# Layer 1's output projection by token groups, and value tiles woven with the last query and key norms

## The chip, the core and the metric

The kernel runs on one core of a Trainium2 chip. The metric is the device time of one execution in microseconds (us). Three runs of the kernel before gave 2983.98, 2985.34 and 2985.49 us; the median is 2985.34. The engines of the core are named as in the profile: PE multiplies matrices, PEld loads its weights, DVE, ACT and POOL work on vectors, SP issues most of the transfers (DMA).

## What is computed

One inference step of a two-layer backbone, for 1024 latent tokens and 128 context tokens together (1152 columns), 1024 features, all in fp32. Layer 0 mixes tokens by pooling and latent attention, layer 1 by neighbourhood attention with 16 heads. Each layer ends with an mlp. Cut to layer 1, where the change lies:

```python
def na_latent(h, k_ctx, v_ctx, w_in, na_q_norm, na_k_norm, rel_bias, w_out):
    q, k, v = na_qkv(h, w_in, na_q_norm, na_k_norm)     # rms norm of each head's q and k
    attn = neighbourhood_attention(q, k, v, k_ctx, v_ctx, rel_bias).reshape(B, S, D_MODEL)
    return attn @ w_out
...
    xs = xs + g1_s * ms
    xs = xs + g2_s * channel_mixer(modulate(xs, norm_mlp[i], sh2_s, sc2_s), mlp1[i], mlp2[i])
```

The context tokens (`xp`) take the same path with plain attention and their own modulation.

## The kernel before

Activations lie with features on the 128 partitions and the 1152 tokens along the free dimension: `x` is 8 tiles of 128x1152. A chunk is 384 tokens (`CH`, three of them) or 288 (`HC`, four). Each fp32 product is made of three products of halves: every operand is split into a rounded high part and a low rest (`wh`, `wl` for weights, `oh`, `ol` for attention outputs), and `mm3` (L329 to L337) issues high x low, low x high, high x high. A tile of the projection over 4 of its 8 input blocks is thus 12 matmuls. A weight block is loaded by SP into `wr`, cast by ACT into `wh` (L160) and subtracted by DVE, or for some weights by POOL, into `wl` (L161); there are 3 buffers of `wr`, and 4 each of `wh` and `wl`.

Python code issues the instructions, partly through generators that `weave` advances in proportion (each with a number of steps). A scheduler of the framework then simulates the program and fixes the order on each engine. Each engine runs its queue in order. PSUM has three pools of banks: `pa` and `pb` with 3, `pc` with 2. SBUF tiles come from a pool `S` of slots, which `S.free` gives back.

The passages that the change touches, in order of time:

1. Queries and keys of layer 1. In four groups `g` of two head pairs each, L1244 and following make the raw products, `square_sum` and `head_rstd` the norm factors `r8h`, `r8l` of the three chunks, and then, for each chunk and each of four tiles, two matmuls (`bcast`, L707 and L708) spread the factors over 128 partitions in a `ps_b` bank, and DVE multiplies (L1266). At the end the results are split (L1270, L1271) and stored to `qd` and `kd`.
2. Values. `value_gen1` makes 36 tiles of 24 matmuls of 256 columns (L1427 to L1429), nine for each quarter of the weights `wv`, and copies them out with ACT (L1433). It is woven with `na_max` (L1320, L1321, L1323) of heads 0 and 1.
3. The heads. Head `h` makes scores `ps_st`, exponents `p`, and values `ps_pv`; `finish_values` copies the outputs of a head pair to `no` and the denominators to `den`, and `recip_pair` (L1082 to L1086) divides. All pairs but the last go to memory (`od`) and come back as `op`.
4. The output projection. In head 15, `split_acts` (L937, L938) splits the first four pairs, and `out_first` makes 24 tiles (8 output blocks, three chunks of 384) over the first four input blocks; `OA` = 8 of them are woven into head 15 after `OW` = 10 empty steps, `OB` = 6 follow while the last pair's division runs. `out_second` makes 32 tiles (four chunks of 288) over the other four. Each tile is added to `x` by DVE, with the gate (L342 in the first, L896 in the second; two instructions where a chunk crosses from latent to context tokens). After chunks 0 and 1 their norm statistics follow, and from chunk 2 on `operand_gen` makes the mlp's operands: modulated `hq` (L311), their products, and the split into `bh` (L352) and `bl` (L353).
5. The mlp. L446 to L448 are the first matmuls of its first product; its weights pass through ACT L419 and DVE or POOL L420.

Layer 0 already has its projection in the form that the change brings to layer 1: `split_groups` (L914, L915) and `out_group`, with the residual in L929.

Of the kernel before, what the change touches and what calls it, by code (L numbers as in the profile page):

```python
# [13 lines left out]
ALU = mybir.AluOpType  # L14
# [18 lines left out]
XS, PSH, OW, OA, OB = (11, 11, 12, 12, 13, 13, 14, 14), (14, 14, 15, 15), 10, 8, 6  # L33
# [57 lines left out]
def hybrid_kernel(ctx: ExitStack, tc: tile.TileContext, I, O):  # L91
# [783 lines left out]

    def out_first(layer, acts):
        for q in range(4):
            ws = wout_chunk(layer, 0, q)
            for mi in range(2):
                for ch in range(NCH):  # L880
                    ps = PS("ps_o")[:, :CH]
                    mm3(ps, ws[mi], acts, ch * CH, ch * CH + CH)
                    residual(x, 2 * q + mi, ch, ps, layer, 0)
                    yield

    def out_second(layer, acts):
        ws = [wout_chunk(layer, 1, q) for q in range(4)]
        st, right, ops, og = {}, [], {}, None
        for ch in range(4):
            for m in range(KD):  # L890
                if ch == 3 or ch == 2 and m in (3, 6):
                    next(og, None)
                ps = PS("ps_o", ("pa", "pc")[m % 2])[:, :HC]
                mm3(ps, ws[m // 2][m % 2], acts, ch * HC, ch * HC + HC)
                for a, b, i in chunk_parts(ch, HC):
                    nc.vector.scalar_tensor_tensor(x[m][:, a:b], ps[:, a - ch * HC:b - ch * HC], adav(layer, 2, m, i),  # L896
                                                   x[m][:, a:b], op0=ALU.mult, op1=ALU.add)
# [33 lines left out]

    def split_acts(ops):
        acts = []
        for o in ops:
            a = (S.alloc("oh", F32R), S.alloc("ol", F32R))
            acts.append(a)
            nc.vector.tensor_copy(a[0], o)  # L937
            nc.vector.tensor_sub(a[1], o, a[0])  # L938
            S.free(o)
        return acts  # L940

    def free_acts(acts):
        for a in acts:
            S.free(*a)
# [288 lines left out]
    r8 = S.alloc("r8h", F32R), S.alloc("r8l", F32R)  # L1233
    silu_load()
    for g in range(4):
# [16 lines left out]
        for ch in range(NCH):  # L1252
            cs = slice(ch * CH, ch * CH + CH)
            ps8 = PS("ps8", "pb")[0:8, :CH]
            for t in range(4):
                square_sum(ps8, t, raw[t][:, cs], t == 0, t == 3)
            head_rstd(ps8, 64, cs, nts[(NCH * g + ch) % 2], r8, rows)
        for ch in range(NCH):
            for t in range(4):
                wn = "naq" if t < 2 else "nak"  # L1260
                pp_ = pq if t < 2 else pk
                ps = PS("ps_b", "pb")[:, :CH]
                bcast(ps, t, r8, slice(ch * CH, ch * CH + CH), rows)
                for a, b, i in chunk_parts(ch):
                    o = pp_[:, pairs[t] * P:pairs[t] * P + P] if i else raw[t][:, a:b]
                    nc.vector.scalar_tensor_tensor(o, raw[t][:, a:b], V(wn), ps[:, a - ch * CH:b - ch * CH],  # L1266
                                                   op0=ALU.mult, op1=ALU.mult)
        for t in range(4):
# [388 lines left out]
```

## Time and profile before

| what | value |
|---|---|
| median of three runs | 2985.34 us |
| the profiled execution | 2996.6 us |
| its span | 2994.7 us |
| mean granted PE clock | 0.977 |

One execution was profiled; all durations below come from it. A timeline row gives start and duration in us, engine, line, operation, output and inputs, partitions x elements and, in brackets, the idle time before it and what ended that. The durations of matmuls overlap, so the distance from start to start is their cost. A row of the windows gives a stretch's bounds and length, busy time and count of instructions for PE, PEld, DVE, ACT and POOL, then PE's granted clock, the DMA share and GB/s.

### The profile page before, as it was taken

Reading aid. Unit: us, or ns where it says so; the run is one execution under the profiler, and the core shown is the slowest. Engines: PE = TensorE matmul, PEld = TensorE weight load, DVE = VectorE, ACT = ScalarE, POOL = GpSimd, SP = SyncE. Lnnn points to the kernel's source line nnn. Section 1 sums busy time; section 2 is a strip of 40 time slices with the busy share of each in tenths; the row PEclk is TensorE's granted clock in tenths of the full one; section 3 lists DMA queues with packets and bytes.
Section 4 is the critical chain, followed back from the end, with each engine's and each line's share of the span. In section 5 each row is a group of like instructions: output and inputs, shape, how many; then the busy total and the mean of one; then the engine's idle time right before and its main releaser. Section 6 shows DMA issues by size and latency. Waiting matters only on the chain. (4 is left out here: it accounts for less than half of the span.)

```text
span 2994.7 us, 46426 instructions
## 1 busy us (share of the span) xinstructions
PE 2909.3 (97%) x18302; PEld 2610.2 (87%) x18302; DVE 2151.7 (72%) x3923; ACT 1321.2 (44%) x2136; POOL 329.3 (11%) x238
## 2 busy tenths in 40 slices
PE   7999999999999999999999999998989999999999
PEld 4955666799999999999988897666989999999999
DVE  5977863477778899786898524667587678877775
ACT  5463444345355544354644423444244445453433
POOL 2004010141000020000221000111020000200000
PEclk9997999999999999999999999898989999999999
DMA  6527521222232344233555325775213222332322
GB/s 236 170 86 254 144 76 41 77 77 88 84 105 77 101 141 148 78 99 92 170 204 183 116 101 128 194 187 165 70 36 99 80 91 85 117 101 78 98 78 89
DMA packets 117435, 347.59 MB, mean 116 GB/s; under 512 B 16697, under 2 KB 37801, under 8 KB 117218
## 3 DMA queue, kind: packets, MB, share of 16 engines
q1 hardware_dynamic: 114674, 340.76, 36.9%
q0 software_dynamic: 2544, 3.87, 0.4%
q8 instruction: 144, 2.36, 0.3%
q14 instruction: 73, 0.60, 0.1%
HBM read 296.54 MB, written 46.85 MB: 115 GB/s over the span
## 5 line engine op out<-in xcount | busy, mean ns | idle before, releaser
L477 PE MATMUL ps<-mh,wl 128*128 128x288 f32 x2048 | 599.8, 294 | 0.0
L478 PE MATMUL ps<-mh,wh 128*128 128x288 f32 x2048 | 595.6, 295 | 0.0
L476 PE MATMUL ps<-ml,wh 128*128 128x288 f32 x2048 | 590.4, 295 | 2.6 <-DVE x L482 1.4
L446 PE MATMUL ps<-bl,wh 128*128 128x288 f32 x1792 | 534.4, 299 | 16.1 <-DVE bl L353 5.2
L447 PE MATMUL ps<-bh,wl 128*128 128x288 f32 x1792 | 530.9, 296 | 0.0
L448 PE MATMUL ps<-bh,wh 128*128 128x288 f32 x1792 | 529.2, 295 | 0.0
L477 PEld LDWEIGHTS ps<-mh,wl 128*128 128x128 f32 x2048 | 384.2, 188 | 0.1
L476 PEld LDWEIGHTS ps<-ml,wh 128*128 128x128 f32 x2048 | 380.1, 188 | 3.6 <-DVE x L482 1.4
L478 PEld LDWEIGHTS ps<-mh,wh 128*128 128x128 f32 x2048 | 382.4, 188 | 0.0
L482 DVE SCALAR_TENSOR_TENSOR x<-ps,ada,x 128x288 f32<-128x288 f32 (+2 forms) x640 | 270.8, 451 | 122.7 <-PE ps L478 121.5
L446 PEld LDWEIGHTS ps<-bl,wh 128*128 128x128 f32 x1792 | 337.9, 189 | 20.5 <-issue 9.3
L448 PEld LDWEIGHTS ps<-bh,wh 128*128 128x128 f32 x1792 | 339.7, 190 | 0.0
L447 PEld LDWEIGHTS ps<-bh,wl 128*128 128x128 f32 x1792 | 338.8, 189 | 0.2
L160 ACT CAST wh<-wr 128x1024 fp32r<-128x1024 f32 x188 | 197.1, 1049 | 190.2 <-PE ps L448 77.3
L419 ACT CAST wh<-s 128x512 fp32r<-128x512 f32 x256 | 146.1, 618 | 278.6 <-PE ps L478 194.9
L161 DVE TENSOR_TENSOR wl<-wr,wh 128x1024 fp32r<-128x1024 f32 x144 | 179.2, 1248 | 60.1 <-ACT wh L160 60.1
L200 DVE CUSTOM_DVE_ANT_0 trash<-wada,silu 128x1024 bf16<-128x1024 f32 x160 | 206.1, 1288 | 13.3 <-DMA wada<-in_wada 6.9
L419 ACT CAST wh<-wr 128x1024 fp32r<-128x1024 f32 (+1 forms) x128 | 106.9, 835 | 199.7 <-PE ps L478 135.7
L161 POOL TENSOR_TENSOR wl<-wr,wh 128x1024 fp32r<-128x1024 f32 x44 | 117.2, 2670 | 689.8 <-ACT wh L160 689.8
L420 DVE TENSOR_TENSOR wl<-s,wh 128x512 fp32r<-128x512 f32 x232 | 157.2, 709 | 3.7 <-ACT wh L419 1.5
L1115 PE MATMUL ps_pv<-p,vt 128*128 128x512 f32 x288 | 147.7, 596 | 0.1
L1074 DVE TENSOR_REDUCE stat<-ps_m 128x1 f32<-128x384 f32 x192 | 98.6, 551 | 65.2 <-PE ps_m L1073 64.9
(321 smaller groups left out, 6044.2 us busy)
## 6 DMA issues: line engine op xcount, KB each, us to landing
wr<-in_w SPq DMA_DIRECT2D x256, 512.0 KB, 3.7
wada<-in_wada SPq DMA_DIRECT2D x48, 512.0 KB, 3.5
wada<-in_wada0t SPq DMA_DIRECT2D x32, 512.0 KB, 3.7
wr<-in_win SPq DMA_DIRECT2D x24, 512.0 KB, 4.5
wr<-in_wout SPq DMA_DIRECT2D x24, 512.0 KB, 4.3
kk<-kd SPq DMA_DIRECT2D x32, 288.0 KB, 7.3
wadan<-in_wada SPq DMA_DIRECT2D x16, 512.0 KB, 8.8
ta<-in_bias_q SPq DMA_DIRECT2D x16, 512.0 KB, 4.4
```

The lines of the kernel that those rows point to most:

```text
L160: nc.scalar.copy(hi, r)
L161: (nc.gpsimd if e else nc.vector).tensor_sub(lo, r, hi)
L200: nc.vector.tensor_tensor_reduce(trash, r[:, :D], silu[i][:, :D], scale=1.0, scalar=0.0, op0=ALU.mult, op1=ALU.add, accum_out=a)
L419: nc.scalar.copy(h, src)
L420: (nc.gpsimd if j in EDGE and min(ps) in EDGE_POOL else nc.vector).tensor_sub(l, src, h)
L446: nc.tensor.matmul(ps, wh[:, a], hl[:, b], start=k == 0, stop=False)
L447: nc.tensor.matmul(ps, wl[:, a], hh[:, b], start=False, stop=False)
L448: nc.tensor.matmul(ps, wh[:, a], hh[:, b], start=False, stop=k == 3)
L476: nc.tensor.matmul(ps, wh, hl, start=kk == 0, stop=False)
L477: nc.tensor.matmul(ps, wl, hh, start=False, stop=False)
L478: nc.tensor.matmul(ps, wh, hh, start=False, stop=kk == 3)
L482: nc.vector.scalar_tensor_tensor(x[m][:, a:b], ps[:, a - ch * HC:b - ch * HC], g, x[m][:, a:b], op0=ALU.mult, op1=ALU.add)
```

## The change

First, the norms of a group become a generator `norm_group`, which yields after each chunk's factors, after each chunk's four multiplications and after each of four stores. `value_gen1` is defined ahead of the loop. For groups 0 to 2 the generator is run through as before; for the last group it is woven with the first nine value tiles. The other 27 value tiles are then woven with `na_max` of heads 0 and 1.

Second, layer 1's operands are split by `split_groups` into two halves of 576 tokens. `out_first` makes chunks 0 and 1 over the first four input blocks, 16 tiles of 288 columns; `OA` becomes 10. `out_second` makes the same two chunks over the other four blocks, with their norm statistics, then gives back the halves of group 0 it holds, and makes chunks 2 and 3 over all eight blocks, in tiles of 24 matmuls, with the weights of both halves loaded again; after every second of these 16 tiles `operand_gen` advances by one step. `split_acts` and `free_acts` go.

```diff
-XS, PSH, OW, OA, OB = (11, 11, 12, 12, 13, 13, 14, 14), (14, 14, 15, 15), 10, 8, 6
+XS, PSH, OW, OA, OB = (11, 11, 12, 12, 13, 13, 14, 14), (14, 14, 15, 15), 10, 10, 6
...
+    def out_tile(layer, m, ch, ws, acts, k):
+        ps = PS("ps_o", ("pa", "pc")[m % 2] if k else "pa")[:, :HC]
+        mm3(ps, ws, acts, ch % 2 * HC, ch % 2 * HC + HC)
+        for a, b, i in chunk_parts(ch, HC):
+            nc.vector.scalar_tensor_tensor(x[m][:, a:b], ps[:, a - ch * HC:b - ch * HC], adav(layer, 2, m, i),
+                                           x[m][:, a:b], op0=ALU.mult, op1=ALU.add)
...
     def out_first(layer, acts):
         for q in range(4):
             ws = wout_chunk(layer, 0, q)
             for mi in range(2):
-                for ch in range(NCH):
-                    ps = PS("ps_o")[:, :CH]
-                    mm3(ps, ws[mi], acts, ch * CH, ch * CH + CH)
-                    residual(x, 2 * q + mi, ch, ps, layer, 0)
+                for ch in range(2):
+                    out_tile(layer, 2 * q + mi, ch, ws[mi], acts, 0)
                     yield
...
     def out_second(layer, acts):
         ws = [wout_chunk(layer, 1, q) for q in range(4)]
-        st, right, ops, og = {}, [], {}, None
-        for ch in range(4):
+        st = {}
+        for ch in range(2):
             for m in range(KD):
-                if ch == 3 or ch == 2 and m in (3, 6):
-                    next(og, None)
...
-            if ch < 2:
-                st[ch] = norm_stats(x, ch, HC)
-            if ch == 1:
-                og = operand_gen(ops, quad_apply(x, 0, layer, st[0]), right)
-            elif ch == 2:
-                right.extend(quad_apply(x, 1, layer, st[1]))
+                out_tile(layer, m, ch, ws[m // 2][m % 2], [a[0] for a in acts[4:]], 1)
+            st[ch] = norm_stats(x, ch, HC)
+        for a in acts[4:]:
+            S.free_ap(a[0][0])
+        ops = {}
+        og = operand_gen(ops, quad_apply(x, 0, layer, st[0]), quad_apply(x, 1, layer, st[1]))
+        n = 0
+        for q in range(4):
+            ws = [wout_chunk(layer, half, q) for half in range(2)]
+            for mi in range(2):
+                for ch in (2, 3):
+                    out_tile(layer, 2 * q + mi, ch, [w for half in range(2) for w in ws[half][mi]], [a[1] for a in acts], 1)
+                    n += 1
+                    if n % 2 == 0:
+                        next(og, None)
         run(og)
...
+        norm = norm_group(g, raw, rows, pairs)
+        if g < 3:
+            run(norm)
+        else:
+            vg = value_gen1()
+            weave((norm, 10), (islice(vg, 9), 9))
...
-    weave((value_gen1(), 36), (chain(na_max(0, tls[0]), na_max(1, tls[1])), 10))
+    weave((vg, 27), (chain(na_max(0, tls[0]), na_max(1, tls[1])), 10))
...
-            acts = split_acts(pairs)
-            of = out_first(1, acts)
+            acts = [split_groups(o) for o in pairs]
+            of = out_first(1, [a[0] for a in acts])
...
-    free_acts(acts)
-    acts = split_acts(pairs + opairs[7:])
+    for a in acts:
+        S.free_ap(a[0][0])
+    acts += [split_groups(o) for o in pairs + opairs[7:]]
     ops = out_second(1, acts)
```

Lines of the changed kernel have other numbers: L1266 becomes L1247, L1427 to L1429 become L1278 to L1280, L1320 becomes L1356, L914 and L915 become L924 and L925, and the residual of layer 1 is L880.

The order of PE's instructions around the last norms, before the change, from the end of the seventh value tile on:

```order
L1428 MATMUL ps_v_16828<-wh,hl_956_13882 128x256
L1429 MATMUL ps_v_16828<-wh,hh_948_13874 128x256
L707 MATMUL ps_b<-r8h_14389,bcs_14365 128x384
L708 MATMUL ps_b<-r8l_14390,bcs_14365 128x384
...
L707 MATMUL ps_b<-r8h_14389,bcs_14365 128x384 x3
L708 MATMUL ps_b<-r8l_14390,bcs_14365 128x384 x3
L707 MATMUL ps_b<-r8h_14389,bcs_14365 128x384
L708 MATMUL ps_b<-r8l_14390,bcs_14365 128x384
L1320 MATMUL ps_m<-kk_16653,qq_16654 128x256
```

And at the same place after it, where `ps_v_16800` is the eighth value tile:

```order
L1279 MATMUL ps_v_16770<-wh,hl_956_13882 128x256
L1280 MATMUL ps_v_16770<-wh,hh_948_13874 128x256
L1278 MATMUL ps_v_16800<-wl,hh_941_13867 128x256
...
L1280 MATMUL ps_v_16800<-wh,hh_943_13869 128x256
L707 MATMUL ps_b<-r8h_14389,bcs_14365 128x384
L708 MATMUL ps_b<-r8l_14390,bcs_14365 128x384
L1278 MATMUL ps_v_16800<-wl,hh_944_13870 128x256
...
L1278 MATMUL ps_v_16800<-wl,hh_946_13872 128x256
L707 MATMUL ps_b<-r8h_14389,bcs_14365 128x384
L708 MATMUL ps_b<-r8l_14390,bcs_14365 128x384
```

The eight broadcast pairs that followed one another now have between 4 and 24 value matmuls between them, and the first `ps_m` comes after two more value tiles.

DVE's queue at the start of the mlp, before (`x_1386` and `x_1404` are blocks of `x`; L452 and L453 are the mlp's first instructions on results):

```order
L896 SCALAR_TENSOR_TENSOR x_1404_19748<-ps_o,ada_92,x_1404_19748 128x160
L353 TENSOR_TENSOR bl_20807<-t_1494_20788,bh_20806 128x1152
L381 TENSOR_TENSOR hq_20769<-hq_20770,hq_20769 128x1152
L896 SCALAR_TENSOR_TENSOR x_1404_19748<-ps_o,ada_92,x_1404_19748 128x128
...
L353 TENSOR_TENSOR bl_20827<-hq_20769,bh_20826 128x1152
L353 TENSOR_TENSOR bl_20846<-t_1493_20787,bh_20845 128x1152
L388 TENSOR_TENSOR hq_20632<-hq_20632,t_1494_20788 128x1152
L452 TENSOR_TENSOR u_20965<-ps_20981,scr_20966 128x288
L453 TENSOR_TENSOR scr_20966<-ps_20995,scr_20966 128x288
L353 TENSOR_TENSOR bl_20866<-hq_20632,bh_20865 128x1152
L353 TENSOR_TENSOR bl_20885<-hq_20770,bh_20884 128x1152
```

And after:

```order
L880 SCALAR_TENSOR_TENSOR x_1386_19630<-ps_o,ada_92,x_1386_19630 128x128
L353 TENSOR_TENSOR bl_21009<-hq_20528,bh_21008 128x1152
L353 TENSOR_TENSOR bl_21066<-hq_20546,bh_21065 128x1152
L880 SCALAR_TENSOR_TENSOR x_1403_19746<-ps_o,ada_92,x_1403_19746 128x288
...
L880 SCALAR_TENSOR_TENSOR x_1403_19746<-ps_o,ada_92,x_1403_19746 128x160
L880 SCALAR_TENSOR_TENSOR x_1403_19746<-ps_o,ada_92,x_1403_19746 128x128
L880 SCALAR_TENSOR_TENSOR x_1404_19748<-ps_o,ada_92,x_1404_19748 128x288
...
L880 SCALAR_TENSOR_TENSOR x_1404_19748<-ps_o,ada_92,x_1404_19748 128x160
L880 SCALAR_TENSOR_TENSOR x_1404_19748<-ps_o,ada_92,x_1404_19748 128x128
```

The last four of seven left operands `bl` stood behind the last residual, two of them behind the mlp's first results; now all seven stand ahead of the residuals of the last two blocks.

DVE's queue in head 15, where the projection's operands are split, before:

```order
L161 TENSOR_TENSOR wl<-wr,wh 128x1024
L938 TENSOR_TENSOR ol_20312<-op_20152,oh_20311 128x1152
L937 CAST oh_19848<-op_19834 128x1152
L937 CAST oh_20307<-op_20151 128x1152
L161 TENSOR_TENSOR wl<-wr,wh 128x1024
L937 CAST oh_20315<-op_20153 128x1152
L938 TENSOR_TENSOR ol_19849<-op_19834,oh_19848 128x1152
L938 TENSOR_TENSOR ol_20316<-op_20153,oh_20315 128x1152
L938 TENSOR_TENSOR ol_20308<-op_20151,oh_20307 128x1152
L342 SCALAR_TENSOR_TENSOR x_1339_19367<-ps_o,ada_92,x_1339_19367 128x384 x2
```

And after (`op_19834` is the operand of which `ol_19849` was made, the first of the three splits in a row above):

```order
L925 TENSOR_TENSOR oa_20204<-op_20190,oa_20204 128x576
L924 CAST oa_19854<-op_19834 128x576
L924 CAST oa_20195<-op_20189 128x576
L924 CAST oa_20207<-op_20191 128x576
L925 TENSOR_TENSOR oa_19854<-op_19834,oa_19854 128x576
L925 TENSOR_TENSOR oa_20195<-op_20189,oa_20195 128x576
L161 TENSOR_TENSOR wl<-wr,wh 128x1024
L925 TENSOR_TENSOR oa_20207<-op_20191,oa_20207 128x576
L924 CAST oa_20210<-op_20191 128x576
L924 CAST oa_20198<-op_20189 128x576
L880 SCALAR_TENSOR_TENSOR x_1339_19367<-ps_o,ada_92,x_1339_19367 128x288 x2
```

The subtraction into `oa_19854` stands behind three casts of other halves, one of them of `op_20191`, the operand that is loaded last.

More of the change, by code (lines that the diff above doesn't have):

```diff
@@ L1233, in hybrid_kernel, with norm_group @@
     r8 = S.alloc("r8h", F32R), S.alloc("r8l", F32R)
+    def norm_group(g, raw, rows, pairs):
+        for ch in range(NCH):
+            cs = slice(ch * CH, ch * CH + CH)
+            ps8 = PS("ps8", "pb")[0:8, :CH]
+            for t in range(4):
+                square_sum(ps8, t, raw[t][:, cs], t == 0, t == 3)
+            head_rstd(ps8, 64, cs, nts[(NCH * g + ch) % 2], r8, rows)
+            yield
+        for ch in range(NCH):
+            for t in range(4):
+                wn = "naq" if t < 2 else "nak"
+                pp_ = pq if t < 2 else pk
+                ps = PS("ps_b", "pb")[:, :CH]
+                bcast(ps, t, r8, slice(ch * CH, ch * CH + CH), rows)
+                for a, b, i in chunk_parts(ch):
+                    o = pp_[:, pairs[t] * P:pairs[t] * P + P] if i else raw[t][:, a:b]
+                    nc.vector.scalar_tensor_tensor(o, raw[t][:, a:b], V(wn), ps[:, a - ch * CH:b - ch * CH],
+                                                   op0=ALU.mult, op1=ALU.mult)
+            yield
+        for t in range(4):
+            hi, lo = fhs[t % 2], raw[t].bitcast(F32R)
+            nc.scalar.copy(hi[:, :NS], raw[t][:, :NS])
+            nc.vector.tensor_sub(lo[:, :NS], raw[t][:, :NS], hi[:, :NS])
+            dst, o = (qd, 0) if t < 2 else (kd, P)
+            dma(dst[0][pairs[t], :, o:o + NS], hi[:, :NS])
+            dma(dst[1][pairs[t], :, o:o + NS], lo[:, :NS])
+            yield
@@ L1251, in hybrid_kernel @@
             background(QBG)
[L1252 to L1268, printed above, removed]
-            hi, lo = fhs[t % 2], raw[t].bitcast(F32R)
-            nc.scalar.copy(hi[:, :NS], raw[t][:, :NS])
-            nc.vector.tensor_sub(lo[:, :NS], raw[t][:, :NS], hi[:, :NS])
-            dst, o = (qd, 0) if t < 2 else (kd, P)
-            dma(dst[0][pairs[t], :, o:o + NS], hi[:, :NS])
-            dma(dst[1][pairs[t], :, o:o + NS], lo[:, :NS])
+        norm = norm_group(g, raw, rows, pairs)
+        if g < 3:
+            run(norm)
+        else:
+            vg = value_gen1()
+            weave((norm, 10), (islice(vg, 9), 9))
         if g == 2:
@@ L1512, in hybrid_kernel @@
     run(of)
-    free_acts(acts)
-    acts = split_acts(pairs + opairs[7:])
+    for a in acts:
+        S.free_ap(a[0][0])
+    acts += [split_groups(o) for o in pairs + opairs[7:]]
     ops = out_second(1, acts)
```

65 lines of the change are left out of this document (24 added, 41 removed).

## The prediction

> **What bounds the kernel now.** I read the page's busy shares and its chain first, then the table of windows, then the single rows of the timeline where TensorE (PE) waits.
>
> ```profile
> span 2994.7 us, 46426 instructions
> PE 2909.3 (97%) x18302; PEld 2610.2 (87%) x18302; DVE 2151.7 (72%) x3923; ACT 1321.2 (44%) x2136; POOL 329.3 (11%) x238
> PE 28%; DVE 1%; DMA 1%; issue 1%; POOL 0%; ACT 0%; SPq 0%; DVEq 0%; POOLq 0%; ACTq 0%
> ```
>
> PE is busy for 97% of the span and the chain that ended last is nearly all PE. So the time falls only where PE waits, or where it runs at less than its full clock. The windows show three such places near the change: around 1720 us (query and key norms of the last pair group), 2100 us (start of layer 1's output projection) and 2210 to 2240 us (its end, start of the mlp).
>
> ```profile
> 1720.00:1730.00 10.00, 7.40 (x26) 6.26 (x27) 8.71 (x21) 3.86 (x6) 1.55 (x4) 0.55 0.36 145
> 1730.00:1740.00 10.00, 10.00 (x78) 9.73 (x77) 4.98 (x10) 4.17 (x6) 2.09 (x5) 0.94 0.97 354
> ...
> 2090.00:2100.00 10.00, 8.34 (x39) 6.59 (x38) 9.56 (x12) 5.38 (x7) 0.77 (x1) 1.00 0.61 220
> 2100.00:2110.00 10.00, 7.68 (x33) 6.61 (x32) 7.97 (x12) 0.00 (x0) 0.00 (x0) 0.83 0.29 105
> ...
> 2180.00:2190.00 10.00, 10.00 (x78) 10.00 (x77) 10.00 (x17) 3.91 (x8) 2.69 (x2) 1.00 0.01 2
> ...
> 2200.00:2210.00 10.00, 9.30 (x70) 9.07 (x69) 10.00 (x14) 7.54 (x12) 9.83 (x5) 1.00 0.16 53
> 2210.00:2220.00 10.00, 4.49 (x17) 4.17 (x18) 9.64 (x10) 1.98 (x3) 2.67 (x1) 0.63 0.35 105
> 2220.00:2230.00 10.00, 9.51 (x53) 9.16 (x52) 6.68 (x8) 4.36 (x7) 3.50 (x3) 0.69 0.01 2
> 2230.00:2240.00 10.00, 7.24 (x45) 7.01 (x44) 7.09 (x10) 4.78 (x6) 2.19 (x2) 0.83 0.19 52
> ```
>
> After the bounds come busy time and count of PE, of its weight loads, of DVE, ACT and POOL, then PE's granted clock, DMA share and GB/s. Busy time hides a slow clock, so I count matmuls. The rows that follow show the full-clock step: 0.13 us from start to start for 288 columns, against 0.24 after a wait.
>
> ```profile
> 2208.88 0.29 PE L447 MATMUL ps<-bh,wl 128*128 128x288 f32 x1
> 2209.01 0.29 PE L448 MATMUL ps<-bh,wh 128*128 128x288 f32 x1
> 2214.54 0.58 PE L446 MATMUL ps<-bl,wh 128*128 128x288 f32 x1 [5.23 <-DVE bl L353]
> 2214.91 0.44 PE L447 MATMUL ps<-bh,wl 128*128 128x288 f32 x1
> 2215.15 0.44 PE L448 MATMUL ps<-bh,wh 128*128 128x288 f32 x1
> ```
>
> Between 2210 and 2240 PE starts 17 + 53 + 45 = 115 such matmuls, 115 x 0.1333 = 15.3 us of full-clock work in 30 us (0.1333 is the mean of the step): 14.7 lost, and 0.9 between 2209.1 and 2210. **Place B costs about 15.6 us.** What ends its first wait is DVE, busy 10.00 and 9.64 of 10: there the mlp's left operand `bl` comes after all else.
>
> **Part 1, values woven with the last norms.** The broadcasts `ps_b` of the last norms stand back to back on PE, and each bank is freed by DVE:
>
> ```profile
> 1715.58 0.28 PE L1428 MATMUL ps_v<-wh,hl 128*128 128x256 f32 x1
> 1715.69 0.28 PE L1429 MATMUL ps_v<-wh,hh 128*128 128x256 f32 x1
> ...
> 1722.32 1.33 PE L707 MATMUL ps_b<-r8h,bcs 8*128 8x384 f32 x3 [2.51 <-DVE r8h L703]
> 1724.89 0.65 PE L707 MATMUL ps_b<-r8h,bcs 8*128 8x384 f32 x1 [0.29 <-DVE pq L1266]
> ```
>
> Of the 26 matmuls of 1720 to 1730, 8 are these broadcasts of 384 columns (0.17 us at full clock, two rows further down: 1.4 us) and 18 have 256 columns (0.12 by the two starts above: 2.2): 3.6 us of work in 10, 6.4 lost. The clock of 0.55 there and 0.94 in the next window are part of that price. The change puts some 70 value matmuls of 256 columns, 8 us of work that exists anyway, between these broadcasts; the first `ps_m` follows later. What is late next is DVE's own chain to `r8h`: nineteen matmuls (2.3 us) stand between the broadcast ahead of it and the one that waited 2.51, so some tenths stay. No matmul is added, the nine tiles leave the later weave, and their weights are loaded earlier on SP's queue ahead of the heads' loads. DMA stood at 0.36 in this window and at 0.97 in the next, so the earlier place has the room. I take **-5**, between -3 (half moves elsewhere) and -6.5 (all); a loss is left out, since the matmuls put in are ready work.
>
> **Part 2, projection by token groups.** PE's columns do not change: before, 24 tiles of 12 matmuls of 384 and 32 tiles of 12 of 288, after 64 tiles' worth of 288: 49.9 + 51.2 = 101 us against 102 us, +1 at most, which I hold within the ends below.
>
> Place B. Chunks 0 and 1 are now finished, and their norm made, before the last third of the projection: 16 tiles of 24 matmuls, 384 x 0.1333 = 51.2 us, in which DVE can make the operands. Layer 0 does this already, and its windows at the same passage show what is left:
>
> ```profile
> 643.00:653.00 10.00, 10.00 (x78) 10.00 (x77) 10.00 (x10) 1.88 (x2) 2.59 (x1) 1.00 0.32 107
> ...
> 663.00:673.00 10.00, 8.85 (x65) 8.41 (x64) 9.38 (x12) 2.81 (x5) 4.99 (x3) 1.00 0.21 64
> ```
>
> 65 x 0.1333 = 8.7 in the second: 1.3 us lost where its mlp begins, at a clock of 1.00. Is there room on layer 1's DVE? Its prices:
>
> ```profile
> 2195.52 3.52 DVE L311 SCALAR_TENSOR_TENSOR hq<-x,ada,nt 128x288 f32<-128x288 f32 x8
> 2211.20 3.19 DVE L353 TENSOR_TENSOR bl<-t,bh 128x1152 fp32r<-128x1152 f32 x1
> 2218.16 1.35 DVE L353 TENSOR_TENSOR bl<-t,bh 128x1152 fp32r<-128x1152 f32 x1
> ...
> L161 DVE TENSOR_TENSOR wl<-wr,wh 128x1024 fp32r<-128x1024 f32 x144 | 179.2, 1248 | 60.1 <-ACT wh L160 60.1
> L160 ACT CAST wh<-wr 128x1024 fp32r<-128x1024 f32 x188 | 197.1, 1049 | 190.2 <-PE ps L448 77.3
> wr<-in_wout SPq DMA_DIRECT2D x24, 512.0 KB, 4.3
> ```
>
> In DVE's new order I count for the third: 5 weight subtractions L161 (6.0 us, a little under 1.25 each when queued), 7 of L353 (1.27 queued: 8.9), 8 of L311 (3.5), four other products of 1152 columns (5.1, as L353), 8 weight products of the mlp and one subtraction of 512 columns (half of L353's size, 0.6 each: 5.4), 24 residual instructions (0.33 in the mean, by L311's 0.44 for 288 columns: 7.9), norm pieces (2.8): about 39.6 us, an estimate from these rows by columns. Two-input instructions beside a busy POOL took 3.19 instead of 1.35; with some 5 us of that I have 45 of 51. It fits: in the new order the last of the mlp's left operands stands ahead of six of the residual instructions. From 15.6 to about 1.6: **-14**, between -11 and -15.
>
> The eight extra loads of `wout` (4.3 us to landing) lie where the DMA share is 0.01 to 0.35, the eight extra ACT casts (1.05 us each) where ACT is busy 3.91 of 10 (2180 to 2190); both at nothing. If that cover went, a tile's weights would be late by up to 5.4 us. Residual instructions fall from 72 to 56, on DVE, off the path.
>
> Place A, start of the projection. Now:
>
> ```profile
> 2093.16 1.12 PE L1358 MATMUL ps_pv<-cp,vt 128*128 128x512 f32 x2 [1.10 <-ACT den L1041]
> ...
> 2097.32 0.33 PE L335 MATMUL ps_o<-ol,wh 128*128 128x384 f32 x1
> 2097.50 0.33 PE L336 MATMUL ps_o<-oh,wl 128*128 128x384 f32 x1
> ...
> 2102.98 0.44 PE L335 MATMUL ps_o<-ol,wh 128*128 128x384 f32 x1 [2.24 <-DVE ol L938]
> 2103.85 0.52 PE L335 MATMUL ps_o<-ol,wh 128*128 128x384 f32 x1
> 2104.17 0.52 PE L336 MATMUL ps_o<-oh,wl 128*128 128x384 f32 x1
> ...
> 2101.57 3.89 DVE L938 TENSOR_TENSOR ol<-op,oh 128x1152 fp32r<-128x1152 f32 x3
> ...
> L915 DVE TENSOR_TENSOR oa<-pooled,oa 128x576 fp32r<-128x576 f32 x8 | 6.1, 759 | 0.3
> ```
>
> DVE splits the operands while PE has little else. The windows from 2090 to 2110 hold 72 matmuls, nearly all of 384 columns: 72 x 0.1733 = 12.5 us in 20, 7.5 lost, with the step at 0.32 after the wait of 2.24, where it was 0.18 before it. The change splits by halves (0.76 for a half's subtraction in layer 0), but DVE's order has both halves of most operands ahead of the first residual, with a cast behind a load of `op` among them, and PE's first tiles are narrower: 27 matmuls of 0.1333 instead of 0.1733 lie ahead of the operand that is late, 3.6 us of cover instead of 4.7. By a tally of DVE's queue that subtraction into `oa` ends near 2103.3; `ol` let PE go at 2102.98. So 1.1 + 0.3 more wait, and about 1 more at the slow step: **+2.5**, between 0 (the halves that come early help as much) and +4.
>
> The last head pair:
>
> ```profile
> 2124.66 0.69 DVE L1040 COPY no<-ps_pv 64x512 f32<-64x512 f32 x1 [1.89 <-PE ps_pv L1380]
> ...
> 2128.31 2.39 POOL L1084 TENSOR_TENSOR den<-den,ry 128x1024 f32<-128x1024 f32 x1 [37.47 <-ACT ry L1083]
> ...
> 2136.38 1.35 DVE L938 TENSOR_TENSOR ol<-no,oh 128x1152 fp32r<-128x1152 f32 x1
> ```
>
> From the copy to the finished split are 13.1 us, hidden by 16 tiles of 12 x 0.1733 = 2.08 us. After the change 95 matmuls (12.7 us) and 0.9 of others stand ahead of that operand's first use, while the first half's split and the shorter queue end about 14.1 after PE's last value product: a wait of 0.5. With what a slow clock may add, **+1**, between 0 and +3; queued behind it on PE is the whole projection.
>
> Sum: -5 - 14 + 2.5 + 1 = **-15.5 us** against the profiled run of 2996.6 (2994.7 of span): 2981.1. That run is 11.3 us above the median of 2985.34, so on the median: 2985.3 - 15.5 = **2970**.
>
> **Rule against row.** The wait of 2.24 us above is followed by steps of 0.32 instead of 0.17 us, and the one of 2.51 by a granted clock of 0.55. The Trainium skill, "TensorE: Matmul & The Clock Gate", section "Why this matters for your kernels", asks for no gaps above some 3 us. By it waits of 1 to 2.5 us at A and the last pair would cost their length alone, and the sum would be near -17, within the forecast's own range. The rows disagree with that figure: shorter waits brought the half clock too.
>
> **Rivals.**
> 1. DVE stays late at B. For: 10.00 of 10 at 643 to 653 in layer 0, and eight L161 more than there, where POOL did them. If contention takes 17 us rather than 5, DVE needs 57, PE waits 6 us and loses some 2 more at the slow step: B gives 15.6 - 8 = 7.6 instead of 14, the total is -9, 2976. Against: layer 0's rows. The Trainium skill, "GPSIMD Engine Reference", section "Specifications", says that POOL shares its SBUF interfaces with VectorE instructions of two SBUF inputs; L353's 3.19 agrees.
> 2. Part 1 only moves its wait: `pa` has three banks, the value copies stand behind ACT's casts, which wait for the norms. Gain -1 instead of -5: 2974. Against: in the new order two value copies precede those casts.
> 3. Slower: DVE pays the shared price through the whole last third. 3.19 / 1.35 = 2.36 times on L353, the four products, the nine of 512 columns and L161, 25.4 us together: 35 more, 74 for 51 of PE. Then PE waits 23 us at B instead of 14, with some 1.6 behind, so B gives +9, and with -5 + 3.5 the sum is +7.5: 2993. It decides from about 67 us of DVE work on, where nothing is gained. Against: POOL would have to be busy throughout; it was at 9.83 in one window and at 2.19 to 3.50 in the others quoted from 2180 on.
> 4. The change does not do what it says: the operands are issued beside the last third, but waits (for an operand slot, for weights) make them as late as before, and the values fill only the first broadcast's gap. Then +3.5 and -1 remain: 2988. Against: the two orders, where values and operands have moved.
>
> **Chances.** Forecast (2964 to 2978) 0.60; rival 1 0.17; rival 2 0.10; rival 3 0.07; rival 4 0.06. A measurement of this kernel can tell about 0.2%, 6 us, from no change. Faster by more (under 2979.4): 0.60 + 0.10 (somewhat over half of rival 1) + 0.10 = 0.80; within: 0.07 + 0.06 = 0.13; slower: 0.07. All good ends together give -6.5 - 15 = -21.5, 2964; all bad ones -3 - 11 + 4 + 3 = -7, 2978. To 2981 the range takes in most of rival 1, to 2961 what the reordered matmuls of head 15 may save: 2961 to 2981.
>
> **What would show it.** Right: near 1720 the clock stays above 0.9 and no `ps_b` waits over 1 us; at the start of layer 1's mlp PE starts over 65 matmuls in each 10 us and L446 waits below 1.5; at head 15 a wait of 3 to 4 us for `oa`. Wrong: a wait for `bl` of some us (rival 1), `ps_v` waiting for ACT (rival 2), DVE at 10 of 10 over 50 us with PE below 9 (rival 3).

## The result, and the profile after

| | median us | lowest to highest | runs |
|---|---|---|---|
| before | 2986.35 | 2983.98 to 2995.87 | 9 |
| after | 2972.81 | 2962.70 to 2980.21 | 9 |

The ratio of after to before is 0.9946, with a 95% interval of 0.9929 to 0.9962: 16 us faster, between 11 and 21. The medians differ by 13.5 us, the means by 15.8. The forecast was 15.5 us faster, 2970 us, in a range of 2961 to 2981. The time came out as forecast, and most terms of the sum did; one wait kept its size but had another cause.

The page of the profiled execution (2962.7 us) begins:

```profile
span 2960.5 us, 46643 instructions
PE 2889.9 (98%) x18398; PEld 2596.1 (88%) x18398; DVE 2154.6 (73%) x3931; ACT 1328.2 (45%) x2144; POOL 329.2 (11%) x238
```

The two profiled spans differ by 34.2 us, more than twice what the timed runs say. So the spans can't be used as they are; the program has to be cut into stages. The view of one tile gives, for each line, the count, the durations in ns (lowest, median, highest) and the first and last start in us. Of before, the value matmuls, the scores for the maxima, the value products of the heads, and the mlp's second product in a window from 2150 to 2300:

```profile
L1427 PE MATMUL ps_v<-wl,hh x288: 277/283/580, 1694.0 to 1820.9; 128*128 128x256 f32 x144
L1320 PE MATMUL ps_m<-kk,qq x128: 271/381/579, 1725.8 to 2073.2; 64*128 64x256 f32 x128
L1380 PE MATMUL ps_pv<-p,vt x320: 271/382/1007, 1824.5 to 2124.2; 128*128 128x256 f32 x64, 128*128 128x384 f32 x64, 128*128 128x128 f32 x32
L476 PE MATMUL ps<-ml,wh x64: 288/295/302, 2254.1 to 2280.7; 128*128 128x288 f32 x64
```

The same four of after:

```profile
L1278 PE MATMUL ps_v<-wl,hh x288: 277/283/387, 1691.1 to 1813.5; 128*128 128x256 f32 x144
L1356 PE MATMUL ps_m<-kk,qq x128: 271/381/580, 1735.2 to 2050.5; 64*128 64x256 f32 x128
L1416 PE MATMUL ps_pv<-p,vt x320: 271/382/848, 1817.1 to 2102.6; 128*128 128x256 f32 x64, 128*128 128x384 f32 x64, 128*128 128x128 f32 x32
L476 PE MATMUL ps<-ml,wh x128: 288/295/302, 2220.0 to 2294.4; 128*128 128x288 f32 x128
```

These bounds make four stages. **Values** run from the first to the last of the first row, **heads** on to the last `ps_m`, **start** (of the projection, in head 15) on to the last value product, and **rest** on to the mlp's second product. In us, for all profiles of this study (the experiments are told below; one timed execution of e3 took 5599.29 us and is left out of its ratio):

| kernel | values | heads | start | rest |
|---|---|---|---|---|
| before | 126.9 | 252.3 | 51.0 | 129.9 |
| before_again | 127.0 | 254.6 | 52.8 | 130.8 |
| e1_values (first part alone) | 122.5 | 246.9 | 50.2 | 130.1 |
| after | 122.4 | 237.0 | 52.1 | 117.4 |
| after_again | 122.5 | 241.4 | 54.0 | 117.5 |
| e2_groups (second part alone) | 127.0 | 242.3 | 48.9 | 117.4 |
| e3_late_halves | 122.5 | 242.4 | 48.4 | 120.2 |
| e4_no_beside | 122.5 | 259.4 | 52.6 | 117.4 |
| e5_behind | 122.5 | 245.9 | 52.3 | 143.0 |
| e6_dve22 | 122.5 | 239.5 | 51.7 | 138.1 |
| e6b_dve11 | 122.5 | 248.5 | 51.5 | 121.9 |
| e7_cp | 122.5 | 246.2 | 50.2 | 117.4 |
| e8_cp_late4 | 122.5 | 245.6 | 50.0 | 120.3 |

Values and rest repeat within 0.1 us in the kernels that share them, but for the rest before the change, which varies by 0.9. Heads vary by 22 us without regard to the kernel. So the change is read from the first and the last column, with the start as a small third. Values fell by 4.5 us. The rest fell by 12.9, from 130.3, the mean of three, to 117.4. The start grew by 1.0, from 51.3, the mean of the first three in the table, to 52.4, the mean of the six profiles that issue their loads in the order of after at this place (after, after_again, e4, e5, e6 and e6b). The sum is -16.4 us, which agrees with the measured -16. The rest of the profiled difference is 15.3 us in the heads, whose code the change leaves alone, and 2.9 us ahead of all of it.

Two of these stages do not hold the same work on both sides. The values do: 938 matmuls in before and in after. But the start holds 117 projection matmuls of 384 columns before, and 144 of 288 after. At the prediction's steps of 0.1733 and 0.1333 us this is 1.1 us less work in the start; the rest has 2.4 us more. So the time lost, an estimate from these counts, grew by 2.1 us in the start and fell by 15.3 in the rest.

The windows of after at the three places (bounds and length, then PE, PEld, DVE, ACT and POOL with their counts, PE's clock, DMA share, GB/s):

```profile
1710.00:1720.00 10.00, 10.00 (x64) 7.93 (x63) 6.60 (x12) 2.32 (x5) 0.00 (x0) 1.00 0.21 53
1720.00:1730.00 10.00, 10.00 (x65) 8.08 (x65) 5.96 (x13) 4.42 (x7) 0.62 (x2) 1.00 0.18 72
...
2070.00:2080.00 10.00, 9.12 (x50) 7.12 (x50) 8.82 (x16) 3.99 (x6) 0.00 (x0) 1.00 0.76 261
2080.00:2090.00 10.00, 6.82 (x36) 6.50 (x37) 8.29 (x14) 1.28 (x2) 0.00 (x0) 0.83 0.20 73
...
2170.00:2180.00 10.00, 10.00 (x77) 10.00 (x76) 10.00 (x12) 3.15 (x4) 5.56 (x3) 1.00 0.24 75
2180.00:2190.00 10.00, 10.00 (x78) 10.00 (x77) 6.79 (x11) 2.16 (x4) 4.55 (x3) 1.00 0.01 3
2190.00:2200.00 10.00, 10.00 (x77) 10.00 (x77) 7.01 (x10) 4.36 (x7) 6.03 (x4) 1.00 0.38 105
2200.00:2210.00 10.00, 9.94 (x73) 9.50 (x73) 8.68 (x12) 6.93 (x10) 2.68 (x2) 1.00 0.33 107
```

Around the last norms PE is busy throughout at a clock of 1.00, where it had started 26 matmuls in ten us at 0.55. At the mlp's start it starts 73 to 78 matmuls in each ten us, where it had started 17, 53 and 45. At the start of the projection it still waits, and the clock of 0.83 is the same as before.

### The profile page after: what moved, and what is told of

It is laid out like the page before. It is cut to its first block, busy times and chain, and to the rows that moved or that the text cites. A ratio compares the mean times of both kernels' runs of the same rounds, so it can differ in the third digit from the quotient of the medians.

```text
span 2960.5 us, 46643 instructions
## 1 busy us (share of the span) xinstructions
PE 2889.9 (98%) x18398; PEld 2596.1 (88%) x18398; DVE 2154.6 (73%) x3931; ACT 1328.2 (45%) x2144; POOL 329.2 (11%) x238
## 5 line engine op out<-in xcount | busy, mean ns | idle before, releaser
L160 ACT CAST wh<-wr 128x1024 fp32r<-128x1024 f32 x196 | 205.3, 1048 | 184.0 <-PE ps L448 77.6
L161 DVE TENSOR_TENSOR wl<-wr,wh 128x1024 fp32r<-128x1024 f32 x152 | 188.9, 1245 | 48.9 <-ACT wh L160 48.8
L161 POOL TENSOR_TENSOR wl<-wr,wh 128x1024 fp32r<-128x1024 f32 x44 | 116.9, 2663 | 700.2 <-ACT wh L160 693.9
L335 PE MATMUL ps_o<-oa,wh 128*128 128x288 f32 x512 | 153.6, 301 | 6.9 <-DVE x L880 3.4
L336 PE MATMUL ps_o<-oa,wl 128*128 128x288 f32 x512 | 153.5, 300 | 0.0
```

The source lines that it names most:

```text
L160: nc.scalar.copy(hi, r)
L161: (nc.gpsimd if e else nc.vector).tensor_sub(lo, r, hi)
L335: nc.tensor.matmul(ps, wh, hl[:, c0:c1], start=k == 0, stop=False)
```

## The experiments

Each kernel was profiled once; e1, e2, e3, e7 and e8 were also timed in five rounds against before. The expectations count the rest from the start of the last group of value products, 0.8 to 0.9 us earlier than the table: their 130.7 and 118.3 are the table's 129.9 and 117.4.

### e1_values and e2_groups: each part alone

e1 keeps the values and undoes the projection:

```diff
-            acts = [split_groups(o) for o in pairs]
-            of = out_first(1, [a[0] for a in acts])
+            acts = split_acts(pairs)
+            of = out_first(1, acts)
```

with `out_first`, `out_second` and `OA` of before. 

> Only the values are woven with the last norms; the projection is as before. If each part acts by itself: about -4.5 us against before (the profiled pair of kernels shows -4.5 between the first value matmul and the last one), no ps_b wait above 1 us and a clock above 0.9 near 1720, and the waits at the projection's start (7 to 8 us) and at the mlp's start (about 16 us) unchanged. Rival, that the wait is only displaced: 0 to -1 us, with the loss found later in the value tiles or at head 0. Rival, that the 14 us by which the heads are shorter in the profiled run of the change belong to this part: -18 us, with the heads shorter in its profile too.

e2 keeps the projection and undoes the values:

```diff
-            vg = value_gen1()
-            weave((norm, 10), (islice(vg, 9), 9))
+            run(norm)
...
-    weave((vg, 27), (chain(na_max(0, tls[0]), na_max(1, tls[1])), 10))
+    weave((value_gen1(), 36), (chain(na_max(0, tls[0]), na_max(1, tls[1])), 10))
```

> Only the projection by token groups; values and norms as before. If each part acts by itself: about -11.5 us against before (-15.8 at the mlp's start, +2 at the projection's start and behind the last head pair, +1 for PE's columns and their steps), with the ps_b wait of 2.5 us and the clock of 0.55 near 1720 still there. Rival, that the heads' shorter time belongs to this part: -26 us.

Measured: e1 2982.68 us against 2986.00, ratio 0.9990 (0.9978 to 1.0002), so -3 us, which alone can't be told from nothing. e2 2971.30 us, ratio 0.9950 (0.9937 to 0.9964), -15 us. The stages are sharper than the times. e1 has values at 122.5 and rest at 130.1; e2 has 127.0 and 117.4. Each part does its own stage and leaves the other's alone. The PE timeline (start, duration, idle time before and its end in brackets) shows the two waits that stayed, first e2's, then e1's:

```profile
1718.42 1.32 PE L707 MATMUL ps_b<-r8h,bcs 8*128 8x384 f32 x3 [2.52 <-DVE r8h L703]
```

```profile
2199.49 0.58 PE L446 MATMUL ps<-bl,wh 128*128 128x288 f32 x1 [5.23 <-DVE bl L353]
...
2218.47 0.40 PE L446 MATMUL ps<-bl,wh 128*128 128x288 f32 x1 [2.35 <-DVE u L458]
```

The rival of shorter heads falls, as neither kernel gained 18 or 26 us. The rival of a displaced wait (0 to -1 us) lies inside e1's interval; here the stages have to decide. The values stage is shorter by some 4.5 us in every kernel with the first part, and head 0's first value product starts 2.4 us behind the last value matmul in all thirteen profiles, so nothing was displaced as far as that. A loss later in the heads could not be seen, since they vary by more.

### before_again and after_again: the same kernels once more

> The kernel before once more, for a second profile. If the 14 us by which the heads (last value matmul to last ps_m) were shorter in the change's profile are the heads' own spread from run to run: this stage lies anywhere from 235 to 260 us, and differs from the 252.5 us of the first profile of the same kernel by some us, with the time spent waiting for q<-mrow going along. If they belong to the change: 252 us again, within 1 us. All other stages repeat within 1 us but for the start of the projection.

> The changed kernel once more. By the same theory the heads' stage differs from the first profile's 237.1 us by some us, mostly upward; the values' stage repeats at 122.5, the stage behind the last value product at 118.3 us. The wait for a bank at the projection's start (3.4 us) returns if DVE's queue sets it; if the late third weight block does, it varies.

Heads came to 254.6 and 241.4 us. Alone, that would leave it open whether the change shortens the heads, as the two kernels stayed apart. But e4, which has the changed code in the heads too, took 259.4. The waits of PE in the heads, in after and in e4 (line and tile, what ended the wait, us in total, times, the longest):

```profile
PE ps_st L1384 <- DMA q<-mrow: 4.3, 3, 3.4
PE ps_m L1356 <- DMA qq<-qd: 4.3, 3, 1.6
```

```profile
PE ps_st L1381 <- DMA q<-mrow: 10.7, 5, 4.6
PE ps_m L1353 <- DMA qq<-qd: 6.6, 4, 2.7
```

8.7 of the 22.4 us between them are waits for these two loads. `q<-mrow` is a row of maxima that is written to memory and read back on POOL's queue. before_again waited only 4.0 us for it and still took 254.6, so this wait isn't the whole of the spread. In this stage PE starts 928 matmuls in both profiles; they keep it busy for 218.1 us in after, at a granted clock of 0.95, and for 232.5 us in e4, at 0.89. The other 14.4 us are thus the same matmuls at a lower clock. Why the waits differ from run to run wasn't followed up. The table has 242.3 with the old values and 259.4 with the new, so no effect of the change on the heads is shown.

### e4_no_beside and e5_behind: operands beside the last tiles

e4 takes the steps of `operand_gen` out of the loop:

```diff
                     out_tile(layer, 2 * q + mi, ch, [w for half in range(2) for w in ws[half][mi]], [a[1] for a in acts], 1)
-                    n += 1
-                    if n % 2 == 0:
-                        next(og, None)
         run(og)
```

> As the change, but operand_gen isn't advanced between the last sixteen tiles, so in program order all operands of the mlp follow the projection. If it is the operands' place beside the last tiles that removed the wait at the mlp's start, it returns, 16 us or more (DVE then has some 20 us of products and splits between the last residual and the last bl), so slower than the change by 14 us or more. Rival, that the token groups and the earlier norm alone do it, the scheduler bringing the operands forward: within 3 us of the change.

Its one time, 2986.50 us, is 14 us above the change's median, just the loss that was expected. It would have been taken for proof. The stages say otherwise: rest took 117.4 us, as in after, and all of the surplus is in the heads (259.4). The rival is right: in program order the operands came last, but the scheduler brought them forward.

e5 therefore orders them by force, with a dependency on the last residual that binds the order on DVE alone:

```diff
+                    behind = out_tile(layer, 2 * q + mi, ch, ...)
+        ops = {}
+        og = operand_gen(ops, quad_apply(x, 0, layer, st[0], behind), quad_apply(x, 1, layer, st[1], behind))
         run(og)
...
-                nc.vector.scalar_tensor_tensor(t, x[k][:, a:b], g, y[:, a - c0:b - c0], op0=ALU.mult, op1=ALU.mult)
+                i_ = nc.vector.scalar_tensor_tensor(t, x[k][:, a:b], g, y[:, a - c0:b - c0], op0=ALU.mult, op1=ALU.mult)
+                if behind is not None:
+                    after(i_, behind)
```

> As the change, but every instruction that makes the mlp's operands is ordered behind the last residual on DVE (the scheduler can't bring them forward, as it could in e4). Read by the stage from the last head's last value product to the mlp's first second-product matmul (130.7 us before, 118.3 after, 118.3 in e4). If DVE's making the operands beside the last tiles is what removed the wait: that stage becomes longer than before the change, 140 us or more (8 of L311, a cast and a subtraction stand ahead of the first operand: 7 us, then one operand each 1.3 us or more behind, at half clock). Rival, that the earlier norm and the order of the tiles do it: 119 to 122 us.

The rest took 143.0 us, 25.6 more than after. PE's waits there:

```profile
2209.92 0.61 PE L448 MATMUL ps<-bl,wh 128*128 128x288 f32 x1 [11.42 <-DVE bl L355]
...
2221.64 0.58 PE L448 MATMUL ps<-bl,wh 128*128 128x288 f32 x1 [3.20 <-ACT scr L453]
...
2235.88 0.61 PE L448 MATMUL ps<-bl,wh 128*128 128x288 f32 x1 [3.03 <-DVE u L460]
```

The first is the wait for `bl`, now twice as long as before's 5.23, and the same two kinds of waits follow it. In e5 all seven operands, and the sixteen instructions L311 that start them, stand behind the last residual; before the change only four operands did, which fits a stage that is even longer than before's. So DVE's making the operands while PE works on the last tiles is what removed the wait at the mlp's start. The early norm makes that possible, and the scheduler does it without being asked.

### e6_dve22 and e6b_dve11: how much room DVE has there

Both add subtractions of two finished operand halves, whose results nobody reads:

```diff
                     n += 1
                     if n % 2 == 0:
+                        for e in range(4):
+                            after(nc.vector.tensor_sub(dm[:, :2 * HC], *acts[e][1]), r)
                         next(og, None)
```

`r` is the residual just issued; in e6b the range is 4 up to `n` = 8 and 0 from there.

> As the change, with 32 subtractions of 576 columns (about 0.7 us each) more on DVE behind the last sixteen tiles' residuals; they change no output. In the new order 18 of them, some 12.5 us, stand ahead of the last left operand. The profile of the change shows DVE busy 43 us of 50 there. If DVE has just the room that was estimated (6 to 8 us): a wait of 2 to 5 us for bl or a residual at the mlp's start, with slow steps behind it, so the stage takes 122 to 127 us instead of 118.3. Rival, that DVE is far from the bound (operands ready 10 us early): 118 to 119 us. Rival, that it is at the bound already: 130 us or more.

The rest took 138.1 us, 20.7 more, for some 22 us of added work, far over the expected 4 to 9. But no wait above 0.9 us came before the mlp's own first results:

```profile
2202.01 0.61 PE L446 MATMUL ps<-bl,wh 128*128 128x288 f32 x1 [3.18 <-DVE u L452]
2213.12 0.40 PE L446 MATMUL ps<-bl,wh 128*128 128x288 f32 x1 [3.16 <-DVE u L458]
2227.14 0.61 PE L446 MATMUL ps<-bl,wh 128*128 128x288 f32 x1 [10.56 <-ACT scr L451]
```

None of them waits for an operand. In DVE's order 14 of the 32 extra instructions stand ahead of the last operand, not the 18 of the expectation, and 17 behind the last residual, most of them among the mlp's first results (`u`, `scr`), which free the banks that PE needs. That made e6 a test of another place than meant, hence e6b.

> e6 again with 16 instead of 32 extra subtractions, all behind the first eight of the last sixteen tiles, so that 15 of them stand ahead of the last left operand and only one behind the last residual; outputs unchanged. In e6 no wait came before the mlp's own first results (u, scr), which had half of the extra work right in their queue. If it was that half that cost: the stage behind the last value product takes 118 to 122 us here, since the room in the last third takes some 8 of the 11 us. Rival, that every us on DVE there costs one (e6 lost 20.6 us for 22): 128 us or more.

Here too 14 stand ahead of the last operand. The rest took 121.9 us: 4.5 us lost for some 11 us of work. By the expectation's count that is some 122.8 us, just above its 118 to 122 and far from the rival's 128. The one wait above 0.9 us is the same 3.18 for `u` (L452). So DVE has room for more than half of 11 us in the last third. The estimate of 45 of 51 us was right: in after DVE is busy for 44.4 of the 51.1 us from 2136.3 to 2187.4, in which the last sixteen tiles run. What doesn't fit shows at the first instruction behind it that PE needs, not at `bl`.

### e3_late_halves, e7_cp, e8_cp_late4: the wait at the projection's start

After still waits there, and here the prediction had named the wrong thing: it expected PE to wait for an operand `oa`. The PE row, then DVE's and ACT's rows of the same time, of after:

```profile
2083.06 0.40 PE L335 MATMUL ps_o<-oa,wh 128*128 128x288 f32 x1 [3.39 <-DVE x L880]
```

```profile
2077.34 1.42 DVE L925 TENSOR_TENSOR oa<-op,oa 128x576 fp32r<-128x576 f32 x2
2079.95 1.23 DVE L161 TENSOR_TENSOR wl<-wr,wh 128x1024 fp32r<-128x1024 f32 x1 [1.18 <-ACT wh L160]
2081.09 0.75 DVE L925 TENSOR_TENSOR oa<-op,oa 128x576 fp32r<-128x576 f32 x1
2081.76 0.82 DVE L924 CAST oa<-op 128x576 fp32r<-128x576 f32 x2
2082.50 1.36 DVE L880 SCALAR_TENSOR_TENSOR x<-ps_o,ada,x 128x288 f32<-128x288 f32 x3
```

```profile
2078.87 1.05 ACT L160 CAST wh<-wr 128x1024 fp32r<-128x1024 f32 x1 [2.59 <-DMA wr<-in_wout]
```

PE waits for a bank of `pa`, that is for the first residual (2082.50). Its tile was ready long before (the twelfth projection matmul starts at 2075.55), but the residual stands in DVE's queue behind L161, which waits for ACT's cast, which waits 2.59 us for the third weight block. SP's rows (its queue of DMA issues), first of before, then of after:

```profile
2084.27 10.37 SPq L113 DMA_DIRECT2D wr<-in_wout  x3
2094.73 0.38 SPq L113 DMA_DIRECT2D op<-od  x1
2095.22 5.58 SPq L113 DMA_DIRECT2D wr<-in_wout  x3
```

```profile
2061.62 0.90 SPq L113 DMA_DIRECT2D wr<-in_wout  x2
2072.08 0.33 SPq L113 DMA_DIRECT2D op<-od  x1
2073.32 8.21 SPq L113 DMA_DIRECT2D wr<-in_wout  x4
```

Before, three weight blocks are issued ahead of that load of `op`; after, two. In both kernels the third one waits for its buffer `wr`, which holds the context exponents `cp` of head 15: it is issued 0.6 to 0.7 us behind the start of the last matmul that reads `cp` (2094.31 before, 2073.32 after). Ahead of `op`, ACT's cast then starts 3.83 us after the issue; behind `op`, 5.55. Three kernels test the two causes, the queue of splits and the late block. e3 splits the second token group's halves later:

```diff
-            acts = [split_groups(o) for o in pairs]
+            acts = [[split_half(o, 0)] for o in pairs]
...
-    acts += [split_groups(o) for o in pairs + opairs[7:]]
+    acts += [[split_half(o, 0)] for o in pairs + opairs[7:]]
+    rest = list(zip(acts, early + pairs + opairs[7:]))
...
                 out_tile(layer, m, ch, ws[m // 2][m % 2], [a[0] for a in acts[4:]], 1)
+                if m % 2 and rest:
+                    a, o = rest.pop(0)
+                    a.append(split_half(o, 1))
+                    S.free(o)
```

> As the change, but only the first token group's halves of the eight operands are split in and behind head 15; the second group's halves are split beside out_second's first sixteen tiles. If DVE's long run of splits ahead of the first residual is what PE waits for at the projection's start (3.4 us there, with the slow step after it some 4.5): 3 to 4.5 us faster than the change, about -19.5 us against before, no wait above 1 us for a bank there; the wait behind the last head pair may grow by 1 us, since other halves' instructions stand between its cast and its subtraction. Rival, that the late load of the third weight block sets that wait: no gain, the same 3 us wait, now ended by wl or wh.

e7 takes `cp` of head 15 out of `wr`:

```diff
-        cp = W("wr", "cp")
+        cs_ = S.alloc("cp") if h == 15 else None
+        cp = cs_[:, :1024] if h == 15 else W("wr", "cp")
```

> As the change, but the context exponents of head 15 lie in a slot of S instead of a wr buffer, so the third weight block of the projection is loaded without waiting for them. If that late block (ACT's cast waited 2.6 us for it, DVE's subtraction 1.2, with the first residuals queued behind) sets the wait for a bank at the projection's start: that wait falls from 3.4 to 4.2 us to below 1.5, the stage from the last ps_m to the last value product from about 51 to 48 us, and the kernel is 2 to 4 us faster than the change, about -19 us against before. Rival, that DVE's sixteen half splits ahead of the first residual set it: a wait of 2 us or more remains, now with DVE busy throughout; within 1 us of the change.

e8 is e7 with e3's later halves for the first four operands alone. 

> e7 and, of e3, only the second halves of the first four operands split later. If the bank wait needs both (weights early, and residuals not behind all splits): no wait above 1.5 us for a bank or for wh at the projection's start, that stage 46 to 47.5 us; behind the last head pair a wait of 1.5 to 2 us instead of 0.5 with slow steps, since one cast and one subtraction stand between (stage 27.5 to 28.5 instead of 26.7). In all 2 to 4 us faster than the change, -18 to -20 us against before. Rival, that the heads' end sets the start of the projection: as e3, within 1 us of the change.

| kernel | start | longest wait at the projection's start | rest | ratio to before |
|---|---|---|---|---|
| after, after_again | 52.1, 54.0 | 3.39, 4.21 (bank) | 117.4, 117.5 | 0.9946 (0.9929 to 0.9962) |
| e3 | 48.4 | 4.30 (`wh`) | 120.2 | 0.9939 (0.9925 to 0.9952) |
| e7 | 50.2 | 1.14 (scores), 1.07 (bank) | 117.4 | 0.9950 (0.9930 to 0.9970) |
| e8 | 50.0 | 3.19 (`q<-mrow`) | 120.3 | 0.9956 (0.9942 to 0.9970) |

In e7 the wait for the bank falls to 1.07 us and the start shortens by 2 to 4 us, though 27 of the 32 instructions that split the halves still stand ahead of the first residual, against 26 in after. e2 says the same without having been meant to. Its projection is that of after, but the scheduler gave it another order on SP:

```profile
2070.77 9.53 SPq L113 DMA_DIRECT2D wr<-in_wout  x3
2080.40 0.38 SPq L113 DMA_DIRECT2D op<-od  x1
2082.28 12.20 SPq L113 DMA_DIRECT2D wr<-in_wout  x4
```

The third block stands ahead of `op` and is issued at 2079.98, while PE still reads `cp` (until 2081.65), so it has another buffer. e2 waited 1.09 us for a bank and 1.13 for `wh`, and its start took 48.9, with 25 of the splits' instructions ahead of the first residual. The six profiles with the order of after waited 3.3 to 4.2 us for that bank. So the late block makes up about two thirds of the wait or more, and the splits alone don't make it. The 1.1 us that is left may be theirs; this is not shown. DVE itself idles for the block for a part of that only, 1.18 us in after and 2.39 in after_again; for the rest it is busy with what stands between.

e3 doesn't separate the two causes. There the first residual stands ahead of the third block's subtraction, and no bank is waited for, but that block also comes sooner: its cast starts 6.8 us behind the first projection matmul, against 8.8 in after and 5.1 in e2. Its longest wait ends at the first projection matmul and is for the cast of the first block, so it isn't the wait for the third block that the expectation's rival meant:

```profile
2074.92 0.58 PE L335 MATMUL ps_o<-oa,wh 128*128 128x288 f32 x1 [4.30 <-ACT wh L160]
```

e3 and e8 lost 2.8 us behind the last head pair, where later halves' instructions stand between that pair's cast and its subtraction. All three kernels were expected to be 2 to 4.5 us faster than the change, and e8's start to take 46 to 47.5 us; it took 50.0. The times of all four kernels are the same within their intervals; none is shown to beat the change. e7 has the better trace by 2 us or so, which five rounds can't resolve beside heads that vary by 22.

## Why the prediction was right, point by point

**Values, -5 forecast, -4.5 measured.** As it said, no `ps_b` waits above 1 us, the clock stays at 1.00 and PE fills the time. The stage that was shortened ends with the last value tile, and head 0 starts at the same distance behind it; e1's start and rest are those of before.

**Mlp's start, -14 forecast.** The rest fell by 12.9. That stage also holds the two terms of loss behind the last head pair and in PE's own work, forecast at +1 and at most +1, so the forecast for it was -12 to -13. It also took over 1.1 us of work from the start, and its narrower tiles cost 1.3 us more; by the counts above the time lost there fell by 15.3 us of the 15.6 that the prediction had counted. The wait itself disappeared whole, better than layer 0's windows had led to expect: no wait above 0.5 us is left in PE's timeline from 2100 to 2240. DVE's work was estimated at 45 of 51 us and was 44.4; e6b shows room for some 6 us. e5 shows that it is this overlap that counts. Rivals 1 and 3 (DVE late by its shared port) didn't come: of the windows from 2100 to 2240, DVE was at 10.00 in one only, with POOL at 5.56, and PE lost nothing.

**The last head pair, +1 forecast.** The wait was 0.47 us, against the 0.5 worked out, and no slow step followed it:

```profile
2115.97 0.40 PE L335 MATMUL ps_o<-oa,wh 128*128 128x288 f32 x1 [0.47 <-DVE oa L925]
```

**The projection's start, +2.5 forecast, with "a wait of 3 to 4 us for `oa`".** The wait was 3.39 and 4.21 us, with the slow step behind it. The stage grew by 1.0 us in the mean, inside the 0 to +4, and by 2.1 when its smaller share of the work is counted. The size of the wait was right and its cause wrong, so the size was luck: no wait for `oa` came at this place. The step that failed is the tally of DVE's queue. It asked only when the subtraction into `oa` would end, near 2103.3, and put the residuals "off the path". What PE waited for was the first residual, behind a weight subtraction L161 in the same queue, which waits for a load. The prediction did not follow SP's order here: the third weight block stood ahead of that `op` load before the change and stands behind it after. With the block ahead of it, in e2 and e7, the wait is 1.1 us.

**The rule weighed.** The Trainium skill, "TensorE: Matmul & The Clock Gate", section "Why this matters for your kernels", asks for no PE gaps over some 3 us. The experiments disagree again with that figure: a gap of 1.87 us was followed by 3.3 us of half clock, and one of 3.30 us by none (last section). The wait of 3.39 us did bring the half clock; that of 0.47 cost its length alone.

## What to carry to other kernels

Cut a profile into stages at instructions that both kernels have, and see which stages repeat, before believing a difference of whole spans: here one run of e4 was slower by just the expected amount for another reason. Where a scheduler sets the order, moving code doesn't test a place; a forced dependency does. In a queue that runs in order, follow what each instruction ahead of the awaited one waits for, back to the queue that issues its load.

## What was not expected of the hardware

Whether a gap brings the step of 0.24 us for 288 columns does not depend on its length alone. In e3 a gap of 1.87 us is followed by nine steps at full speed, then by fourteen slow ones, 3.3 us in all:

```profile
2117.99 0.40 PE L335 MATMUL ps_o<-oa,wh 128*128 128x288 f32 x1 [1.87 <-DVE oa L937]
2118.23 0.29 PE L336 MATMUL ps_o<-oa,wl 128*128 128x288 f32 x1
...
2119.45 0.45 PE L336 MATMUL ps_o<-oa,wl 128*128 128x288 f32 x1
2119.69 0.45 PE L337 MATMUL ps_o<-oa,wh 128*128 128x288 f32 x1
...
2122.57 0.39 PE L337 MATMUL ps_o<-oa,wh 128*128 128x288 f32 x1
2122.80 0.30 PE L335 MATMUL ps_o<-oa,wh 128*128 128x288 f32 x1
```

In e6b a gap of 3.30 us, the same wait for a bank that brought slow steps in after, is followed by none:

```profile
2097.69 0.41 PE L335 MATMUL ps_o<-oa,wh 128*128 128x288 f32 x1 [3.30 <-DVE x L880]
2097.93 0.30 PE L336 MATMUL ps_o<-oa,wl 128*128 128x288 f32 x1
2098.07 0.30 PE L337 MATMUL ps_o<-oa,wh 128*128 128x288 f32 x1
```

The gap costs its length, and in most cases here some 1.5 us more: 14 slow steps, give or take one, each 0.107 longer, follow the gaps of 1.87 us (e3), 1.88 (e8), 2.35 (e1), 3.30 (e5), 3.39 (after) and 4.21 (after_again). The Trainium skill, "TensorE: Matmul & The Clock Gate", section "What's actually happening", says that activity is watched in a window of 3.4 us that runs freely. By that it matters where in the window a gap falls; the length of the slow stretch and the two gaps above fit it. Why a gap of 1.87 us, little more than half a window, is enough is shown by no run here.

The second surprise is the heads' stage: 237.0 to 259.4 us over thirteen profiles, while the values ahead of it repeat within 0.1 us. A part of it is waits for rows that go through memory, and a part is the same matmuls at a lower granted clock; what makes either differ from run to run is open.
